# Moving work off the waits of a two-layer decoder trunk, and narrowing its last block

## The chip, the cores and the metric

The kernel runs on one core of one Trainium2 chip. A time is the device time of one execution in microseconds (us); several runs of the same kernel are summed up by their median. The profile comes from one execution of its own, taken by the hardware profiler. Engines are named as in it: PE is TensorE's matmuls, PEld its weight loads, DVE is VectorE, ACT is ScalarE, POOL is GpSimd, SP is SyncE, which issues the DMA transfers. An engine takes its instructions strictly in the order in which they stand in its queue.

## The reference, cut to what matters

One sequence of 1024 tokens with 1024 features goes through a Mamba-2 layer, a shared K/V projection, a stick-breaking attention layer and a last RMS norm:

```python
c_act = silu(c)
shift, scale, gate = split(c_act @ ada_w[0] + ada_b[0], 3)
h = rmsnorm(x, norm_g[0]) * (1 + scale) + shift
zxbcdt = h @ m_in_w                        # z 2048, x/B/C 3072, dt 32
xbc = silu(causal_dwconv(xbc) + conv_b)    # 4 taps
y = ssd_chunked(xs, dt, -exp(a_log), B, C) # 8 chunks of 128, 32 heads
#   per chunk: exp(acum_t - acum_s) below the diagonal * (C B^T), times xs
y = groupnorm((y + d_skip * xs) * silu(z)) * m_norm_g
x = x + gate * (y @ m_out_w)
k, v = split(modulate(x, kv...) @ kv_w, 2)
q, z = split(modulate(x, ada 1...) @ sb_in_w, 2)
x = x + gate1 * ((stick_breaking(q, k, v) * silu(z)) @ sb_out_w)
return rmsnorm(x, final_g)
```

All of it is in float32. The modulation products are the rows of `c_act @ ada_w`.

## The kernel before, in words

Every large product is split in three: an operand is rounded to a short float32 form (`hi`, a cast on ACT) and its remainder (`lo`, a subtraction on DVE or POOL), and `mm3` (L128 to L131) adds hi\*hi, hi\*lo and lo\*hi in PSUM. Weights come as tiles of 128 x 1024 by `load_w` (L116 to L126): a DMA into a raw buffer, the cast on L123, the subtraction on L124. PE takes a weight load of 128 columns before every matmul.

**Start** (L198 to L349). The order of PE, ACT, POOL and DVE is written out by hand here. The rows of x come in eight tiles of 128 tokens, `xn[0]` to `xn[7]`. `squares` (L200) sums the squares of one tile, on ACT or on DVE by its number; `rms` turns four sums into factors, `scaled` (L217) applies them. Per slice of 128 features `d` and half of the tokens `hf`, `turn` (L252) transposes on PE, `high` (L258) applies the modulation and rounds on ACT, `low` (L266) subtracts on DVE, and `wave_mm` (L270) multiplies with the first three weight tiles. `gemv` (L224) makes one slice of shift and scale on DVE, `bias` (L245) finishes it on ACT. `spin` (L210) issues matmuls whose result is overwritten.

**Convolution** (L341 to L458). 24 column tiles of x, B and C: 48 matmuls of 512 columns each, then `conv` (L345): one ACT operation, three on DVE, a SiLU on ACT (L353), a store. `ada_rest(i)` (L357) makes the other six modulation vectors, each from eight DMAs of 512 KB, on DVE (L366) or on POOL and ACT (L363, L364). A scheduler places these instructions by the program's order, what is ready, and its own estimate of durations.

**Scan** (L461 to L640). PE's order is by hand, the other engines' by the scheduler. `chunk_a` (L495) loads a 128 x 8 x 128 tile `lm` of sums of dt\*a, masks it on POOL (L512), and takes eight exponentials of 128 x 128 on ACT (L515); then it is multiplied with C B^T (L534). `chunk_b` (L537) uses it as an operand of `yd` (L545). `lm` has three buffers, so the first three chunks' tiles are loaded ahead. SiLU and the exponential use different ACT tables; a change costs an `ACT_TABLE_LOAD`.

**Attention and the end** (L752 to L1037). The last product with `wso` goes in three blocks of tokens, (half, first column, last column): (1, 0, 512), (0, 0, 256), (0, 256, 512). In a block, for each of eight feature tiles: 24 matmuls into `ps`, a DVE operation that adds the residual (L1009), a square on ACT (L1016), a sum on POOL (L1018). Then a product with ones (L1026, L1027), `inv_rms` (two on ACT, three on DVE), and the scaling: by `finish` (L961) beside the next block, and for the last block by three instructions at L1033, one on POOL and two on DVE, each with its output DMA (L1035).

Of the kernel before, what the change touches and what calls it, by code (L numbers as in the profile page):

```python
# [24 lines left out]
HT = T // NH  # L25
# [27 lines left out]
def tile_trunk(ctx, tc, xT, xN, c, vec, ada0, adar, wxbc, wwave, wdt, wz, wmo, wk, wv, wq, wqz, wso, out):  # L53
# [104 lines left out]
    with ExitStack() as es:  # L158
# [41 lines left out]
        def squares(t):  # L200
            sq = tp.tile([P, D], F32, tag="sq", name=f"sq{t}", bufs=2)
            acc = ssq[:, t // CPH, t % CPH:t % CPH + 1]
            if t % 2:
                V.scalar_tensor_tensor(out=sq, in0=xn[t], scalar=1.0, in1=xn[t], op0=ALU.mult,
                                       op1=ALU.mult, accum_out=acc)
            else:
                S.activation(sq, xn[t], AF.Square, accum_out=acc)
# [67 lines left out]
        def unit(d, hf):  # L275
            high(d, hf)
            low(d, hf)
# [11 lines left out]
        for t in range(CPH):  # L289
# [5 lines left out]
        gemv(0)  # L295
        V.scalar_tensor_tensor(out=vv("b_sc0"), in0=vv("b_sc0"), scalar=1.0, in1=vv("g0"), op0=ALU.add,
                               op1=ALU.mult)
        bias(0)
        unit(0, 0)
        wave_mm(0, 0)  # L300
        spin(xn[0][:, 0:HT], 3)
        for t in range(CPH, NC_):
            squares(t)
        rms(1)
        for t in range(CPH, NC_):
            scaled(t)
# [142 lines left out]
        for n, m in enumerate(todo):  # L449
            wh, wl = wnext if n == 0 else load_w(wxbc[m], f"x{m}")  # L450
            ps = pp.tile([P, T], F32, tag="pr", name=f"pr{m}")
            for k in range(ND):
                for hf in range(NH):
                    mm3(ps[:, hf * HT:(hf + 1) * HT], wh[:, k, :], wl[:, k, :], *h0[k][hf],
                        k == 0, k == ND - 1)
            conv(m, ps)
            if n >= 3 and n % 3 == 0 and n // 3 <= 6:
                ada_rest(n // 3 - 1)  # L458

# [2 lines left out]
    with ExitStack() as es:  # L464
# [32 lines left out]
        def chunk_a(u, c):  # L497
            g, xg, bt, ct = u["g"], u["xg"], u["bt"], u["ct"]
            n = f"{g}_{c}"
            h0_ = HPG * g  # L500
            hsl = slice(h0_, h0_ + HPG)
            cs = slice((c % CPH) * P, (c % CPH + 1) * P)
            sh3 = [P, HPG, P]
            r0 = c * 32 + h0_
            lm = pq.tile(sh3, F32, tag="lm", name="lm" + n, bufs=3)
            Y.dma_start(out=lm, in_=ac_d[r0:r0 + 8, :].rearrange("h t -> (h t)").partition_broadcast(P)
                        .rearrange("p (h t) -> p h t", t=P))
            eb = pq.tile([P, 4, P], F32, tag="eb", name="eb" + n, bufs=1)
            ev = ea_d[r0:r0 + 8, :].rearrange("(j a) t -> a j t", a=2)
            for a in range(2):  # L510
                Y.dma_start(out=eb[64 * a:64 * a + 64], in_=ev[a].partition_broadcast(64))
            Q.affine_select(out=lm, in_=lm, pattern=[[0, HPG], [1, P]], compare_op=ALU.is_ge,  # L512
                            fill=-1e30, base=0, channel_multiplier=-1)
            for h in range(HPG):
                S.activation(lm[:, h, :], lm[:, h, :], AF.Exp, bias=nac[:, c, h0_ + h:h0_ + h + 1])  # L515
            px = ppt.tile([P, 512], F32, tag="px", name="px" + n)
            for j in range(4):
                E.transpose(px[:, j * P:(j + 1) * P], xg[:, j, cs], ident)
            pb = ppt.tile([P, 512], F32, tag="pb", name="pb" + n, bufs=2)
            E.transpose(pb[:, 0:P], bt[:, cs], ident)  # L520
            E.matmul(pb[:, P:2 * P], bt[:, cs], ct[:, cs], start=True, stop=True)
            px3 = px.rearrange("p (h k) -> p h k", k=64)
            xd = pq.tile([P, HPG, 64], F32, tag="xd", name="xd" + n)
            V.tensor_tensor(out=xd, in0=px3, op=ALU.mult,
                            in1=dtv[:, c, hsl].unsqueeze(2).to_broadcast([P, HPG, 64]))
            sp = {}
            if c < NC_ - 1:
                xw = py.tile([P, HPG, 64], F32, tag="xw", name="xw" + n)
                V.tensor_tensor(out=xw, in0=px3, op=ALU.mult,
                                in1=wdv[:, c, hsl].unsqueeze(2).to_broadcast([P, HPG, 64]))  # L530
                sp["xw"] = xw.rearrange("p h k -> p (h k)")
                sp["bs"] = py.tile([P, P], F32, tag="bs", name="bs" + n)
                S.copy(sp["bs"], pb[:, 0:P])
            V.tensor_tensor(out=lm, in0=pb[:, P:2 * P].unsqueeze(1).to_broadcast(sh3), in1=lm, op=ALU.mult)  # L534
            return sp, xd, lm, eb
# [410 lines left out]
    with ExitStack() as es:  # L946
# [23 lines left out]
        w7 = load_w(wso[:, :, 7, :].rearrange("d p c -> p d c"), "s7")  # L970
        done = iter(())
        for hf, c0, c1, ds in ((1, 0, 512, (0, 5, 1, 2, 3, 4, 6, 7)), (0, 0, 256, (6, 7, 0, 1, 2, 3, 4, 5)),
                               (0, 256, 512, (6, 7, 0, 1, 2, 3, 4, 5))):
            w = c1 - c0
            last = hf == 0 and c0 > 0
            n = f"{hf}_{c0}"
            sh = [P, w]
            sqs = pf.tile(sh, F32, tag="sqs", name="sqs2_" + n)
            pss = pp.tile([P, HT], F32, tag="ss", name="ss2_" + n)[:, 0:w]
            x2 = []  # L980
            if hf == 0:
                x2t = pf.tile([P, 8, w], F32, tag="x2q", name="x2_" + n)
            for i, d in enumerate(ds):
                if hf == 0:
                    t = x2t[:, i, :]
                elif d < NPRE:
                    t = x2p[d]
                else:
                    t = pf.tile(sh, F32, tag=f"x2_{d}", name=f"x2_{d}", bufs=1)
                if hf == 0 or d >= NPRE:  # L990
                    Y.dma_start(out=t, in_=x1_d[d][hf][:, c0:c1])
                if hf == 1 and d == NPRE:
                    ps = part[d][0]
                elif hf == 1 and d < NPRE:
                    ps = mm_tile(f"ps{d}_{n}")
                else:
                    ps = pp.tile([P, HT], F32, tag="pq", name=f"ps{d}_{n}", bufs=4)[:, 0:w]
                if hf == 1 and d < NPRE:
                    mm3(ps, w7[0][:, d, :], w7[1][:, d, :], *gg[1][7], True, True)
                elif hf == 1 and d == NPRE:  # L1000
                    mm3(ps, part[d][1][:, 7, :], part[d][2][:, 7, :], *gg[1][7], False, True)
                else:
                    if d not in wos:
                        keep_w(d)
                    wh, wl = wos[d]
                    for k in range(ND):
                        h, l = gg[hf][k]
                        mm3(ps, wh[:, k, :], wl[:, k, :], h[:, c0:c1], l[:, c0:c1], k == 0, k == ND - 1)
                V.scalar_tensor_tensor(out=t, in0=ps, scalar=mod[:, GA1, d:d + 1], in1=t, op0=ALU.mult,  # L1009
                                       op1=ALU.add)  # L1010
                x2.append(t)
                if i == 0:
                    S.activation(sqs, t, AF.Square)
                else:
                    sq = pf.tile(sh, F32, tag="sq", name=f"sq2_{d}_{n}")
                    S.activation(sq, t, AF.Square)  # L1016
                    if i < ND - 1:
                        Q.tensor_tensor(out=sqs, in0=sqs, in1=sq, op=ALU.add)  # L1018
                if last:
                    S.activation(t, t, AF.Identity, scale=vv("gfin", d))  # L1020
                if hf == 1 and d == 4:
                    tc.keep_in_program_order(S.preload_act_table_set("natural_log_exp_and_others"))
                    for k in range(7):
                        load_gs(0, k)
                next(done, None)
            E.matmul(pss, ones, sqs, start=True, stop=False)  # L1026
            E.matmul(pss, ones, sq, start=False, stop=True)  # L1027
            r = pf.tile(sh, F32, tag="rb", name="rb2_" + n)
            inv_rms(pss, r, pf.tile(sh, F32, tag="sq", name="rt2_" + n), D)
            done = finish(hf, c0, c1, ds, x2, r)  # L1030
        for eng, i0, i1 in ((Q, 0, 2), (V, 2, 5), (V, 5, 8)):
            m = i1 - i0
            eng.tensor_tensor(out=x2t[:, i0:i1, :], in0=x2t[:, i0:i1, :],  # L1033
                              in1=r.unsqueeze(1).to_broadcast([P, m, w]), op=ALU.mult)
            Y.dma_start(out=out[ds[i0]:ds[i0] + m, :, c0:c1].rearrange("d p t -> p d t"),  # L1035
                        in_=x2t[:, i0:i1, :])
# [68 lines left out]
```

## Time and profile before

| what | value |
|---|---|
| median of 3 runs | 1477.11 us (1475.7 to 1477.21) |
| the profiled execution: time, span | 1481.88 us, 1480.2 us |
| PE busy | 1442.3 us, 97% of the span |
| PEld busy | 1112.3 us, 75% |
| DVE busy | 957.2 us, 65% |
| ACT busy | 726.7 us, 49% |
| POOL busy | 520.4 us, 35% |
| mean granted TensorE clock | 0.992 |

The span runs from the first to the last instruction that the profile shows. Busy time of PE says that matmuls are in flight, not how close together they are. The granted clock is a share of 2.4 GHz; 0.5 is 1.2 GHz.

### The profile page before, as it was taken

The page shows a single profiled execution, that of the slowest core. Times are in us where ns is not written, and L with a number is a line of the kernel's source. Part 1 is how long each engine was busy: PE and PEld are TensorE (multiplying, and loading weights), DVE is VectorE, ACT ScalarE, POOL GpSimd, SP SyncE. Part 2 cuts the span into 40 slices and gives each one's busy share as a digit, 9 for nine tenths or more (in the row PEclk, how much of TensorE's full clock was granted, in tenths as well). Part 3 has the DMA queues.
Part 4 walks back from the last instruction along what each step waited for, and adds up shares of the span by engine and source line. Part 5 has one row for each costly group of instructions (what it writes and reads, how often), then busy time and mean ns, then how long its engine had stood idle before and what let it go on. Part 6 is the DMA issues. An engine that isn't in the chain of part 4 may idle for free.

```text
span 1480.2 us, 20539 instructions
## 1 busy us (share of the span) xinstructions
PE 1442.3 (97%) x7580; PEld 1112.3 (75%) x7580; DVE 957.2 (65%) x1196; ACT 726.7 (49%) x1218; POOL 520.4 (35%) x602
## 2 busy tenths in 40 slices
PE   6999998999999999999999999999999999999997
PEld 3777886888777777778888888876666666666797
DVE  5688984454789889975733427326656665667564
ACT  6654535334666666733523325235545554555452
POOL 0012220001555655431011000037666666667532
PEclk9999999999999999999999999999999999999999
DMA  9368885224577766567433446441120212112253
GB/s 351 120 217 288 295 294 177 86 100 123 188 231 241 236 219 211 195 196 267 153 119 127 150 122 200 140 156 44 51 79 30 76 47 64 38 58 79 87 184 107
DMA packets 103395, 227.34 MB, mean 154 GB/s; under 512 B 9344, under 2 KB 40832, under 8 KB 102272
## 3 DMA queue, kind: packets, MB, share of 16 engines
q1 hardware_dynamic: 103296, 226.03, 45.8%
q8 instruction: 60, 0.98, 0.3%
q14 instruction: 39, 0.32, 0.1%
HBM read 184.32 MB, written 41.68 MB: 153 GB/s over the span
## 4 chain that ended last, share of the span: by engine, by line
PE 78%; DVE 3%; DMA 1%; ACT 1%; issue 1%; POOL 0%; DVEq 0%; SPq 0%; POOLq 0%; ACTq 0%
PE sc L829 5%; PE av L882 5%; PE at L861 4%; PE po L131 4%; PE po L130 4%; PE po L129 4%; PE pz L131 3%; PE pz L129 3%; PE pz L130 3%; PE pqz L129 2%; PE pq L129 2%; PE pr L131 2%; PE pq L131 2%; PE pr L129 2%; PE pr L130 2%; PE pq L130 2%
## 5 line engine op out<-in xcount | busy, mean ns | idle before, releaser
L852 POOL TENSOR_TENSOR be<-be,kp 128x1024 f32<-128x1024 f32 (+2 forms) x96 | 162.4, 1692 | 90.1 <-DVE kp L846 70.9
L832 ACT ACTIVATE kp<-sc 128x1024 f32<-128x1024 f32 (+2 forms) x96 | 75.6, 813 | 174.4 <-PE sc L829 171.8
L846 DVE TENSOR_TENSOR_SCAN kp<-kp,pone 128x128 f32<-128x128 f32 (+3 forms) x128 | 96.1, 802 | 69.2 <-POOL kp L839 69.2
L129 PE MATMUL pr<-h0h,hx 128*128 128x512 f32 x336 | 132.8, 395 | 7.1 <-ACT hx L123 4.0
L131 PE MATMUL pr<-h0h,lx 128*128 128x512 f32 x336 | 133.2, 396 | 1.4 <-DVE lx L124 1.4
L130 PE MATMUL pr<-h0l,hx 128*128 128x512 f32 x336 | 132.5, 394 | 0.0
L129 PE MATMUL pz<-h0h,hz 128*128 128x512 f32 x256 | 113.0, 441 | 0.0
L131 PE MATMUL po<-yh,lo 128*128 128x512 f32 x256 | 100.0, 391 | 1.3 <-DVE lo L124 1.3
L130 PE MATMUL po<-yl,ho 128*128 128x512 f32 x256 | 100.9, 394 | 0.3 <-DVE yl L659 0.3
L131 PE MATMUL pz<-h0h,lz 128*128 128x512 f32 x256 | 100.5, 393 | 0.1
L130 PE MATMUL pz<-h0l,hz 128*128 128x512 f32 x256 | 100.1, 391 | 0.0
L129 PE MATMUL po<-yh,ho 128*128 128x512 f32 x256 | 100.0, 391 | 0.0
L363 POOL TENSOR_TENSOR ar<-ar,crow 128x1024 f32<-128x1024 f32 x12 | 31.5, 2628 | 186.4 <-DMA ar<-adar 152.6
L846 DVE TENSOR_TENSOR_SCAN kp<-kp,ab,pone 128x512 f32<-128x512 f32 x64 | 78.3, 1265 | 28.3 <-ACT kp L832 17.2
L515 ACT ACTIVATE lm<-lm,nac 128x128 f32<-128x128 f32 x256 | 78.6, 390 | 36.3 <-POOL lm L512 35.9
L550 POOL TENSOR_TENSOR sd<-st,eev 128x512 f32<-128x512 f32 x24 | 39.4, 1641 | 133.7 <-ACT st L562 121.0
L124 POOL TENSOR_TENSOR lq<-rq,hq 128x256 fp32r<-128x256 f32 x32 | 22.4, 730 | 177.8 <-ACT hq L123 177.8
L829 PE MATMUL sc<-kd,q 64*128 64x512 f32 (+3 forms) x384 | 81.5, 522 | 0.8 <-ACT be L833 0.8
L350 DVE SCALAR_TENSOR_TENSOR cv<-pr,vt,cv 128x1023 f32<-128x1023 f32 (+2 forms) x63 | 80.3, 1277 | 0.9
L129 PEld LDWEIGHTS pr<-h0h,hx 128*128 128x128 f32 x336 | 64.2, 191 | 21.6 <-ACT hx L123 4.4
L512 POOL TENSOR_SCALAR_AFFINE_SELECT lm<-lm 128x1024 f32<-128x1024 f32 x32 | 40.3, 1260 | 113.2 <-DMA lm<-ac_d 84.4
L861 PE MATMUL at<-ident,be 128*128 128x128 f32 x576 | 74.7, 272 | 1.2 <-DVE aT L871 1.2
(257 smaller groups left out, 3814.2 us busy)
## 6 DMA issues: line engine op xcount, KB each, us to landing
ar<-adar SPq DMA_DIRECT2D x48, 512.0 KB, 5.6
lm<-ac_d SPq DMA_DIRECT2D x32, 512.0 KB, 4.8
rz<-wz SPq DMA_DIRECT2D x32, 512.0 KB, 3.6
ro<-wmo SPq DMA_DIRECT2D x32, 512.0 KB, 3.6
xs_d<-sv SPq DMA_DIRECT2D x24, 512.0 KB, 3.8
rx<-wxbc SPq DMA_DIRECT2D x21, 512.0 KB, 4.6
a<-ada SPq DMA_DIRECT2D x8, 1024.0 KB, 10.2
xg<-xs_d SPq DMA_DIRECT2D x8, 1024.0 KB, 5.8
```

The source lines that it names most:

```text
L129: E.matmul(ps, wh, xh, start=first, stop=False)
L130: E.matmul(ps, wh, xl, start=False, stop=False)
L131: E.matmul(ps, wl, xh, start=False, stop=last)
L350: V.scalar_tensor_tensor(out=ac[:, i:], in0=ps[:, :T - i], scalar=vv("cw", m * 4 + 3 - i), in1=ac[:, i:], op0=ALU.mult, op1=ALU.add)
L512: Q.affine_select(out=lm, in_=lm, pattern=[[0, HPG], [1, P]], compare_op=ALU.is_ge, fill=-1e30, base=0, channel_multiplier=-1)
L515: S.activation(lm[:, h, :], lm[:, h, :], AF.Exp, bias=nac[:, c, h0_ + h:h0_ + h + 1])
L829: E.matmul(ps[:, a, o:o + w], q[hsl[a], i * P:(i + 1) * P], kd[hsl[a], HT * c:HT * c + w], start=True, stop=True)
L832: S.activation(kp[:, :, ok:ok + w], ps[:, :, o:o + w], AF.Sigmoid, scale=-0.125)
L846: V.tensor_tensor_scan(out=ka, data0=ka, data1=pone.to_broadcast([P, w]), initial=1.0 if top else above[p, i][:, a, 0:1], op0=ALU.mult, op ...
L852: Q.tensor_tensor(out=be[:, :, o:o + w], in0=be[:, :, o:o + w], in1=kp[:, :, ok + 1:ok + w + 1], op=ALU.mult)
L861: E.transpose(ps[:, j, :], be[:, a, j * P:(j + 1) * P], ident)
L882: E.matmul(ps[hsl[a], cs], vd[:, j, hsl[a]], at[j // 4][:, a, j % 4, cs], start=j == 0, stop=j == nj - 1)
```

## The change

It has four parts. The squares of x tiles 4 and 5 go ahead of the first `bias`, those of tiles 6 and 7 between `high` and `low`, and tile 5 goes from DVE to ACT. The exponentials of the first three scan chunks keep their place in the program's order, behind the convolution. The calls of `ada_rest` stand behind other column tiles. The last block of 256 tokens becomes two of 128, with the last scaling in two DVE instructions instead of one on POOL and two on DVE.

```diff
         def squares(t):
-            if t % 2:
+            if t in (1, 3, NC_ - 1):
                 V.scalar_tensor_tensor(out=sq, in0=xn[t], scalar=1.0, in1=xn[t], op0=ALU.mult,
                                        op1=ALU.mult, accum_out=acc)
...
+        for t in (CPH, CPH + 1):
+            squares(t)
         bias(0)
-        unit(0, 0)
+        high(0, 0)
+        for t in (CPH + 2, CPH + 3):
+            squares(t)
+        low(0, 0)
         wave_mm(0, 0)
         spin(xn[0][:, 0:HT], 3)
-        for t in range(CPH, NC_):
-            squares(t)
         rms(1)
...
             conv(m, ps)
-            if n >= 3 and n % 3 == 0 and n // 3 <= 6:
-                ada_rest(n // 3 - 1)
+            if n in (5, 8, 11, 13, 15, 17):
+                ada_rest((5, 8, 11, 13, 15, 17).index(n))
...
             for h in range(HPG):
-                S.activation(lm[:, h, :], lm[:, h, :], AF.Exp, bias=nac[:, c, h0_ + h:h0_ + h + 1])
+                e = S.activation(lm[:, h, :], lm[:, h, :], AF.Exp, bias=nac[:, c, h0_ + h:h0_ + h + 1])
+                if g == 0 and c < 3:
+                    tc.keep_in_program_order(e)
...
-                               (0, 256, 512, (6, 7, 0, 1, 2, 3, 4, 5))):
+                               (0, 256, 384, (6, 7, 0, 1, 2, 3, 4, 5)), (0, 384, 512, tuple(range(8)))):
             w = c1 - c0
-            last = hf == 0 and c0 > 0
+            last = hf == 0 and c1 == HT
...
-        for eng, i0, i1 in ((Q, 0, 2), (V, 2, 5), (V, 5, 8)):
+        for eng, i0, i1 in ((V, 0, 4), (V, 4, 8)):
             m = i1 - i0
             eng.tensor_tensor(out=x2t[:, i0:i1, :], in0=x2t[:, i0:i1, :],
                               in1=r.unsqueeze(1).to_broadcast([P, m, w]), op=ALU.mult)
```

Line numbers in the changed kernel are higher by 3 behind the start, and by 5 behind the exponentials.

ACT's queue at the start, before; `sq` are the squares of an x tile, `mod` is `bias(0)`, `hx` and `h0h` are `high(0, 0)`, `rst` begins `rms(1)`:

```order
L233 CAST wwh_263<-ww_185 128x384
L246 ACTIVATE mod<-mod,vt 128x1
L248 ACTIVATE mod<-mod,vt 128x1
L260 ACTIVATE hx_0_0_272<-xp_0_250,mod 128x512
L263 CAST h0h_0_274<-hx_0_0_272 128x512
L207 ACTIVATE sq_290,ssq<-x_174 128x1024
L207 ACTIVATE sq_294,ssq<-x_176 128x1024
L139 ACTIVATE rst<-ssq,epsb 128x4
```

And of the change:

```order
L233 CAST wwh_263<-ww_185 128x384
L207 ACTIVATE sq_270,ssq<-x_174 128x1024
L207 ACTIVATE sq_272,ssq<-x_175 128x1024
L246 ACTIVATE mod<-mod,vt 128x1
L248 ACTIVATE mod<-mod,vt 128x1
L260 ACTIVATE hx_0_0_276<-xp_0_250,mod 128x512
L263 CAST h0h_0_278<-hx_0_0_276 128x512
L207 ACTIVATE sq_281,ssq<-x_176 128x1024
L139 ACTIVATE rst<-ssq,epsb 128x4
```

Two squares now stand ahead of `mod`, and one instead of two between `h0h` and `rst`; of DVE's two squares one is left, ahead of its `h0l`.

ACT's queue in the convolution, before; `sv` is a tile's SiLU, `lm_0` to `lm_2` are the exponentials of the first three chunks, `hx` is the cast of the next weights:

```order
L353 ACTIVATE sv_1569<-cv_1564 128x1024
L515 ACT_TABLE_LOAD
L515 ACTIVATE lm_0_2388<-lm_0_2388,nac 128x128 x8
L123 CAST hx_1727<-rx_1725 128x1024
L348 ACTIVATE cv_1627<-pr_1578,vt 128x1024
L515 ACTIVATE lm_1_2507<-lm_1_2507,nac 128x128 x8
L515 ACTIVATE lm_2_2583<-lm_2_2583,nac 128x128 x8
L353 ACT_TABLE_LOAD
L353 ACTIVATE sv_1632<-cv_1627 128x1024
L123 CAST hx_1790<-rx_1788 128x1024
```

In the change these exponentials stand at the start of the scan, between the casts of the z weights (`hz`) and the copies of z out of PSUM (`sz`):

```order
L482 COPY sz_0_2322<-pz_0_1_2362 128x512
L518 ACT_TABLE_LOAD
L518 ACTIVATE lm_0_2388<-lm_0_2388,nac 128x128 x8
L538 COPY bs_0_2416<-pb_0_2409 128x128
L123 CAST hz_0_0_2493<-rz_0_0_2491 128x1024
L518 ACTIVATE lm_1_2507<-lm_1_2507,nac 128x128 x3
L482 COPY sz_0_2322<-pz_0_2_2425 128x512
L518 ACTIVATE lm_1_2507<-lm_1_2507,nac 128x128 x5
L123 CAST hz_0_1_2569<-rz_0_1_2567 128x1024
L518 ACTIVATE lm_2_2583<-lm_2_2583,nac 128x128 x3
L482 COPY sz_0_2322<-pz_0_3_2457 128x512
L518 ACTIVATE lm_2_2583<-lm_2_2583,nac 128x128 x5
```

A table load, the SiLU of z and another table load follow. In the convolution nothing stands between the SiLU and the next cast any more. POOL's, DVE's and SP's queues in the convolution have the same instructions in the same order in both kernels, those of `ada_rest` among them.

PE's queue at the end, before: the last matmuls of the block of 256 and its product with ones.

```order
L130 MATMUL ps_0_256_12667<-gl_0_11900,hs_12392 128x256
L131 MATMUL ps_0_256_12667<-gh_0_11899,ls_12393 128x256
L1026 MATMUL ss_0_256_12435<-sqs_0_256_12434,ones 128x256
L1027 MATMUL ss_0_256_12435<-sq_5_0_256_12693,ones 128x256
L1100 UNCONDITIONAL_BRANCH
```

And of the change, at the place where the first block of 128 hands over to the second:

```order
L131 MATMUL ps_0_384_12703<-gh_0_12029,ls_12203 128x128
L129 MATMUL ps_0_384_12703<-gh_0_12035,hs_12202 128x128
L130 MATMUL ps_0_384_12703<-gl_0_12036,hs_12202 128x128
L1031 MATMUL ss_0_256_12435<-sqs_0_256_12434,ones 128x128
L131 MATMUL ps_0_384_12703<-gh_0_12035,ls_12203 128x128
```

The 192 matmuls of 256 columns behind the block (0, 0, 256) have become 384 of 128 columns, with one more pair of products with ones. On SP eight loads of 128 x 128 for the second block follow the stores of the block (0, 0, 256).

## Rows read from the trace of the kernel before

**Rows 1.** The page, chain of work that ended last: shares of the span by engine

```profile
PE 78%; DVE 3%; DMA 1%; ACT 1%; issue 1%; POOL 0%; DVEq 0%; SPq 0%; POOLq 0%; ACTq 0%
```

**Rows 2.** Waits of PE: for whom, us in total, times, longest

```profile
PE pr L129 <- ACT hx L123: 4.0, 1, 4.0
PE prw L129 <- ACT h0h L263: 3.5, 2, 2.0
PE prw L130 <- DVE h0l L268: 2.8, 5, 1.4
PE pr L131 <- DVE lx L124: 1.4, 1, 1.4
```

**Rows 3.** Timeline of ACT, start: start us, us, instruction [idle before <-releaser]

```profile
18.61 0.39 ACT L246 ACTIVATE mod<-mod,vt 128x1 f32<-128x1 f32 x1 [3.00 <-DVE vt L296]
...
21.72 1.06 ACT L207 ACTIVATE sq<-x 128x1024 f32<-128x1024 f32 x1
...
23.87 0.30 ACT L139 ACTIVATE rst<-ssq,epsb 128x4 f32<-128x4 f32 x1 [1.00 <-DVE sq L204]
```

**Rows 4.** Timeline of DVE and PE at the first wave

```profile
30.41 0.69 DVE L268 TENSOR_TENSOR h0l<-hx,h0h 128x512 fp32r<-128x512 f32 x1
...
31.15 0.80 PE L130 MATMUL prw<-h0l,wwh 128*128 128x512 f32 x1 [1.42 <-DVE h0l L268]
...
36.87 0.45 PE L129 MATMUL prw<-h0h,wwh 128*128 128x512 f32 x1
```

**Rows 5.** Timeline of ACT in the convolution

```profile
223.66 1.06 ACT L353 ACTIVATE sv<-cv 128x1024 f32<-128x1024 f32 x1 [2.79 <-issue]
...
230.33 2.44 ACT L515 ACTIVATE lm<-lm,nac 128x128 f32<-128x128 f32 x8 [4.31 <-POOL lm L512]
232.68 1.03 ACT L123 CAST hx<-rx 128x1024 fp32r<-128x1024 f32 x1
```

**Rows 6.** Timeline of PE, the same place

```profile
222.11 0.39 PE L129 MATMUL pr<-h0h,hx 128*128 128x512 f32 x1
...
229.36 0.39 PE L131 MATMUL pr<-h0h,lx 128*128 128x512 f32 x1
233.76 0.50 PE L129 MATMUL pr<-h0h,hx 128*128 128x512 f32 x1 [4.01 <-ACT hx L123]
...
241.61 0.47 PE L129 MATMUL pr<-h0h,hx 128*128 128x512 f32 x1
```

**Rows 7.** Windows of 2 us: busy time per engine (instructions), granted clock, DMA

```profile
236.00:238.00 2.00, 2.00 (x5) 1.61 (x6) 1.97 (x2) 2.00 (x8) 0.00 (x0) 0.50 0.53 141
```

**Rows 8.** DMA issues from 205 to 222 us: KB each, median us to landing

```profile
rx<-wxbc SPq DMA_DIRECT2D x2, 512.0 KB, 4.4
```

**Rows 9.** The chain in order of time, start of the scan: start us, us, what

```profile
353.01 1.02 PE yd L545 x16
...
362.39 1.09 PE yo L555 x8
```

**Rows 10.** Timeline of PE, matmuls of 256 columns in the last block

```profile
1469.09 0.28 PE L129 MATMUL ps<-gh,hs 128*128 128x256 f32 x1
1469.21 0.28 PE L130 MATMUL ps<-gl,hs 128*128 128x256 f32 x1
```

**Rows 11.** Timeline of PEld, two weight loads at the head of a group

```profile
1007.70 0.19 PEld L129 LDWEIGHTS pq<-h1h,hq 128*128 128x128 f32 x1
1007.81 0.19 PEld L130 LDWEIGHTS pq<-h1l,hq 128*128 128x128 f32 x1
```

**Rows 12.** Timeline of the end, all engines

```profile
1469.65 0.48 DVE L1009 SCALAR_TENSOR_TENSOR x<-ps,mod,x 128x256 f32<-128x256 f32 x1 [2.40 <-PE ps L131]
...
1473.38 0.42 DVE L146 SCALAR_TENSOR_TENSOR rb<-rt,rb 128x256 f32<-128x256 f32 x1
...
1473.88 2.03 POOL L1033 TENSOR_TENSOR x<-x,rb 128x512 f32<-128x512 f32 x1 [5.24 <-DVE rb L146]
```

**Rows 13.** Groups by line, L1033: ns min/median/max, first and last start

```profile
L1033 DVE TENSOR_TENSOR x<-x,rb x2: 958/1486/2015, 1473.8 to 1474.7; 128x768 f32<-128x768 f32 x2
```

## The prediction

> **What bounds the kernel now.** I read the chain of work that ended last first: 78% of the span is PE, and no other engine has more than 3% [rows 1]. The kernel is one long row of matmuls. A change can win time where PE stands still or runs at the half clock, or where it needs fewer or cheaper matmuls; it can lose where it makes them dearer. Next I read for whom PE waits: the longest single wait is 4.0 us for an ACT cast of weights, `hx` L123, and behind it come 3.5 us in two waits for `h0h`, 2.8 us in five for `h0l`, and 1.4 us for `lx` [rows 2]. All of these lie at the start and in the convolution. Then I read each place of the change in the timeline of the engines there.
>
> **Pace of PE.** From the matmul at 222.11 to that at 229.36 [rows 6] there are 32, so one of 512 columns takes 7.25/32 = 0.227 us. In the last block the starts of two matmuls of 256 columns lie 1469.21 − 1469.09 = 0.12 us apart [rows 10].
>
> **The first scan exponentials.** On ACT the cast `hx` at 232.68 stands behind eight exponentials at 230.33, and these waited 4.31 us for POOL's mask of `lm` [rows 5]. So PE, which needs the cast, stood from 229.59 to 233.76 (its wait is given as 4.01 us, and the matmul at 229.36 would have been followed 0.23 us later) [rows 6]. That is 4.17 us. What follows is dearer still: from 233.76 to 241.61 PE issued 15 matmuls in 7.85 us [rows 6], where 15 × 0.227 = 3.41 would do; the granted clock there is 0.50, that is 1.2 GHz [rows 7]. That is 4.44 us more. With the exponentials gone from here the cast can follow the SiLU, which ends at 223.66 + 1.06 = 224.72 [rows 5]. Its raw weights are there: of the two transfers the median lands 4.4 us after its issue, the issues lie from 205 to 222 us [rows 8], and this tile's was issued before 222, seven us ahead of its use. So `hx` ends at some 225.8, the subtraction some 1.4 us later, ahead of 229.59. I take both parts, 4.17 + 4.44 = **8.6 us**. The lower bound is the waits alone, 4.0 + 1.4 = 5.4 us [rows 2], if the clock falls in spite of that; the upper is 8.8, with the wait for `lx` beside it.
>
> The same 24 exponentials then cost 3 × 2.44 = 7.3 us on ACT at the start of the scan, and the two table loads move with them. PE's chain there passes through `yd` from 353.01 and `yo` at 362.39 [rows 9]; the first needs `lm` of chunk 0. In ACT's new order these eight stand right behind the second copy of z, ahead of the copy of the first chunk's B, so they come well before 353; those of chunks 1 and 2 stand between casts and copies of z that PE needs later. What hides them is the z product, which PE works through in that time. I cost the place at nothing; the bounds are 0 and 8.6, which is what the same instructions cost where they stood (rival C).
>
> **The other modulation products.** The queues of POOL, DVE and SP in the convolution are the same in both kernels, and what waits there is data from the same transfers. 0 us: this part does not do what its lines say.
>
> **The start.** ACT waits 3.00 us, until 18.61, for `vt` from DVE [rows 3]. Two squares of 1.06 us with 0.1 between them fit in, since x tiles 4 and 5 have landed. Of the two on ACT that stood behind `high`, one is left, and of the two on DVE one. Before, `rms(1)` began at 23.87 after 1.00 us of waiting for DVE's second square [rows 3]. Now DVE's one square ends about 20.3 and ACT's third about 21.7, one square earlier, so `rms(1)` begins at 21.75: 2.1 us earlier. What waits for it on PE is the second half of the tokens: PE waited 1.42 us for `h0l` until 31.15 [rows 4]. This `h0l` also hangs on `gemv(1)` on DVE, which frees earlier by one square, so I take 1.8 of the 2.1 us. The matmul at 36.87 still takes 0.45 us, that at 222.11 took 0.39 and the one at 31.15 took 0.80 [rows 4, 6]: I read the stretch from 31 to 37 as the half clock. About 11 matmuls at 0.43 against 0.227 lose 2.2 us; if the idle time ahead of them shrinks, part of that comes back. Between 1.8 and 1.8 + 2.2 I take **3.0 us**; the bounds are 1.0 (a later wait takes the rest) and 5.
>
> **The last block.** Removed are 8 × 24 = 192 matmuls of 256 columns, 192 × 0.120 = 23.04 us. Added are 2 × 8 × 24 = 384 of 128 columns, each with a weight load of its own as before. The weights are the same, so they are loaded twice. The price of one has no row with this type and width. From below: columns alone. 256 columns more cost 0.227 − 0.120 = 0.107 us, so 128 fewer than 256 cost 0.0535 less, 0.0665. From above: `yo`, eight f32 matmuls of 128 columns in 1.09 us [rows 9], where one product takes two of these, is 0.2725 a product. Between them: the weight load. Two at the head of a group, with no matmul to wait for, start 1007.81 − 1007.70 = 0.11 us apart [rows 11], and a load stands before each matmul whatever its width. At 256 columns the load hides under 0.120; at 128 it is the longer of the two. I take 0.110: 384 × 0.110 = 42.24, so **+19.2 us**. The bounds of the whole are thus +2.5 (0.0665) and +81.6 (0.2725); the nearest row is the load's, and if what goes with it lets the pace be 0.107 to 0.120 the term is +18.0 to +23.0. The extra product with ones is four f32 matmuls of 0.11: **+0.45**. The eight extra loads of x on SP stand behind the stores of block (0, 0, 256) and are wanted only some 20 us later, behind the first block of 128: hidden.
>
> The Trainium skill ("TensorE: Matmul & The Clock Gate", section "Back-to-back issue gap") gives about 81 ns for each matmul of 128 columns in a sustained stream of load and matmul pairs; the trace has no such stream of this width, and by that figure the estimate would be 384 × 0.081 = 31.1 us, +8.1 in place of +19.2, and the sum −5.6, about 1471.5. It speaks against the 0.110 of the loads, which is a row of this kernel, and the row decides.
>
> **The end.** Behind the last matmul stand, for 256 columns, the residual (0.48), square, product, two on ACT, and three of DVE at 0.42 [rows 12]. With 128 columns each of DVE's drops by some 0.15 (its first scaling took 0.958 for 768 columns [rows 13], 0.16 for 128): four times that is 0.6, and I add 0.4 for ACT's three and PE's product, which shrink alike: 1.0 us. The scaling: DVE's two of 768 columns took 0.958 and 2.015, the second beside POOL's one of 2.03 [rows 12, 13]; together 2.97 us. Now two of 8 × 128 / 2 = 512 columns each run without POOL: 2 × 0.958 × 512/768 = 1.28, with a little between them 1.4. That is 1.5 us less. Together **2.5 us**; bounds 1.5 (DVE keeps its mean pace of 1.49 per 768, so 2.0 for both) and 3.5.
>
> **Sum.** −8.6 − 3.0 + 19.2 + 0.45 − 2.5 = **+5.55 us**. Against the profiled execution's own 1481.88 that is 1487.4. This execution lies 4.77 us above the median of the runs, 1477.11; the same step from there gives 1482.7.
>
> **Rivals.**
> A: narrow matmuls go by their columns. PE would start the next 128 columns while the load for a later one is under way, and loads come faster than the 0.11 us seen at a group's head. Price 0.0665: 384 × 0.0665 = 25.5, +2.5, and the sum is −11.2: 1465.9, faster. For it: at 256 and 512 columns pace goes by columns. Against it: loads at least 0.11 apart [rows 11]; it decides from a pace under 0.0955 us, where 384 × 0.0955 − 23.04 = 13.65 eats up what the other terms (−8.6 − 3.0 − 2.5 + 0.45) save.
> B: narrow products cost what f32 products do, 0.2725 each: 384 × 0.2725 = 104.6, +81.6, and about +68: 1545. For it: the only matmuls of 128 columns with float32 operands in the trace go so [rows 9]. Against it: those are of the full type in two passes, these of the short one in one.
> C: the exponentials cost PE at the start of the scan what they cost in the convolution. `lm` of chunk 0 is then later than 353.01 or the state copies later than 362.39 [rows 9]; the gain of 8.6 is gone and the sum is +14.15: 1491.3. Against it: ACT's order, in which chunk 0's eight come first.
>
> **How the numbers follow.** Forecast .70, A .15 (with prices between 0.0665 and 0.09), B .07, C .08. What a measurement can tell from no change is 0.2%, 2.95 us. The forecast's own range: load-bound pace +18 to +23, exponentials −8.8 to −5.4, start −5 to −1, end −3.5 to −1.5; not all at one end, 1478 to 1492. To hold 8 in 10, the range goes down to 1462 for most of A and up to 1493 for C; B is left out. Faster: A and the gain end of the forecast, .20. Slower: most of the forecast, B, C, .71. Within: .09.
>
> **What would show it.** Right: in the convolution no PE wait for `hx` near 229 us, and no clock of 0.50 near 236; `rms(1)` about 2 us earlier and PE's first wait for `h0l` shorter; in the two blocks of 128 matmul starts 0.11 us apart, the stretch of both 42 us long with PEld busy throughout; the scaling at the end in 1.4 us. Wrong: starts 0.07 apart (A) or 0.27 (B); a new wait of `yd` or `yo` for ACT between 340 and 365 us (C); or a wait for `hx` or `lx` at the next tile that takes the place of the one removed, which would show as a PE gap of over 1 us between 230 and 260 us.

## The result and the profile after

| comparison | before, median (runs) | changed, median (runs) | ratio, 95% interval |
|---|---|---|---|
| first | 1477.16 us (4) | 1488.11 us (4) | 1.0073, 1.0057 to 1.0089 |
| second, on another chip | 1477.39 us (23) | 1488.58 us (6) | 1.0065, 1.0047 to 1.0083 |

The changed kernel is slower by some 11 us, 0.7%. The forecast said slower, by 5.55 us: the direction and the largest term were right, the size was half. Between the two profiled executions the difference is 1485.9 − 1480.2 = 5.7 us, as forecast; between the medians it is twice that. The profiled execution of before was a long one (1481.88 us against a median of 1477.16), which the first experiment shows in its stages.

The chain of work that ended last in the changed kernel, shares of the span (before in [rows 1]):

```profile
PE 88%; DVE 6%; ACT 2%; DMA 2%; issue 2%; POOL 0%; SPq 0%; DVEq 0%; ACTq 0%; POOLq 0%
```

PE's waits, in total, times, longest. The wait for the cast `hx` (4.0 in [rows 2]) and that for `lx` are not among them any more; `h0h` has 1.8 instead of 3.5, `h0l` 1.6 instead of 2.8. The longest in the convolution is now a single wait of 2.9 us for `cv`, the convolution on DVE; it is not new, before it came to 3.1 us in two:

```profile
PE pr L129 <- DVE cv L353: 2.9, 1, 2.9
PE prw L129 <- ACT h0h L263: 1.8, 2, 1.5
PE prw L130 <- DVE h0l L268: 1.6, 5, 0.4
```

The start in the timeline of the changed kernel. ACT fits two squares into its wait (0.90 us are left of the 3.00 in [rows 3]), `rst` begins at 21.69 and not at 23.87, and PE's matmul that waited for `h0l` until 31.15 [rows 4] starts at 28.97:

```profile
16.54 1.04 ACT L207 ACTIVATE sq<-x 128x1024 f32<-128x1024 f32 x1
...
18.57 0.39 ACT L246 ACTIVATE mod<-mod,vt 128x1 f32<-128x1 f32 x1 [0.90 <-DVE vt L296]
...
21.69 0.30 ACT L139 ACTIVATE rst<-ssq,epsb 128x4 f32<-128x4 f32 x1
...
28.97 0.50 PE L130 MATMUL prw<-h0l,wwh 128*128 128x512 f32 x1 [0.43 <-DVE h0l L268]
```

The convolution, where PE stood for the cast [rows 5, 6]. The SiLU is followed by a cast with nothing between, and this cast is already that of the tile after; PE runs on at 0.227 us, with the clock at 1.00 in the window that had 0.50 in [rows 7]:

```profile
223.21 1.06 ACT L356 ACTIVATE sv<-cv 128x1024 f32<-128x1024 f32 x1 [4.07 <-issue]
225.53 1.05 ACT L123 CAST hx<-rx 128x1024 fp32r<-128x1024 f32 x1 [1.25 <-PE pr L130]
...
226.01 0.39 PE L131 MATMUL pr<-h0h,lx 128*128 128x512 f32 x1
226.23 0.39 PE L129 MATMUL pr<-h0h,hx 128*128 128x512 f32 x1
```

```profile
236.00:238.00 2.00, 2.00 (x10) 1.67 (x9) 0.51 (x1) 1.59 (x2) 0.00 (x0) 1.00 0.00 0
```

The narrow blocks. Matmuls of 128 columns start 0.11 to 0.12 us apart, as do their weight loads, where those of 256 columns took 0.12 [rows 10]. At the change-over the loads keep their distance (1433.34, 1433.46, 1433.57), but the second narrow matmul starts only 0.06 us behind the first; from then on the matmuls follow their loads. From the first (1433.46) to the last (1477.49) it is 44.03 us for 384; before it was 23.78 for 192. The mean is 44.03/384 = 0.115, which contains the products with ones between them; without those it is 0.112, the median 0.111:

```profile
1433.46 0.22 PE L129 MATMUL ps<-gh,hs 128*128 128x128 f32 x1
1433.52 0.28 PE L130 MATMUL ps<-gl,hs 128*128 128x128 f32 x1
1433.63 0.27 PE L131 MATMUL ps<-gh,ls 128*128 128x128 f32 x1
...
1477.15 0.28 PE L131 MATMUL ps<-gh,ls 128*128 128x128 f32 x1
1477.20 0.19 PEld L129 LDWEIGHTS ps<-gh,hs 128*128 128x128 f32 x1
1477.26 0.28 PE L129 MATMUL ps<-gh,hs 128*128 128x128 f32 x1
1477.32 0.19 PEld L130 LDWEIGHTS ps<-gl,hs 128*128 128x128 f32 x1
1477.38 0.27 PE L130 MATMUL ps<-gl,hs 128*128 128x128 f32 x1
...
1477.49 0.27 PE L131 MATMUL ps<-gh,ls 128*128 128x128 f32 x1
```

The last scaling, two of 512 columns without POOL beside them, takes 1.29 us; before, the two of 768 took 0.958 and 2.015 [rows 13], with POOL's at work beside both (1473.88 to 1475.91 [rows 12]):

```profile
L1038 DVE TENSOR_TENSOR x<-x,rb x2: 685/688/692, 1481.0 to 1481.6; 128x512 f32<-128x512 f32 x2
```

### The profile page after: what moved, and what is told of

Its sections match the earlier page's. It is cut to its first block, busy times and chain, and to the rows that moved or that the text cites. A ratio compares the mean times of both kernels' runs of the same rounds, so it can differ in the third digit from the quotient of the medians.

```text
span 1485.9 us, 21021 instructions
## 1 busy us (share of the span) xinstructions
PE 1458.6 (98%) x7776; PEld 1131.0 (76%) x7776; DVE 957.1 (64%) x1213; ACT 728.7 (49%) x1230; POOL 518.4 (35%) x607
## 3 DMA queue, kind: packets, MB, share of 16 engines
q8 instruction: 62, 1.02, 0.3%
## 4 chain that ended last, share of the span: by engine, by line
PE 88%; DVE 6%; ACT 2%; DMA 2%; issue 2%; POOL 0%; SPq 0%; DVEq 0%; ACTq 0%; POOLq 0%
PE sc L834 5%; PE av L887 5%; PE pr L129 4%; PE pr L131 4%; PE pr L130 4%; PE at L866 4%; PE po L131 4%; PE po L130 4%; PE po L129 4%; PE pz L129 3%; PE pz L130 3%; PE pz L131 3%; PE pqz L129 2%; PE pq L129 2%; PE pq L131 2%; PE pq L130 2%
```

## The experiments

Times of before vary from 1471 to 1485 us in these comparisons, so each run stands against before in the same comparison, by its ratio. The diffs are against before unless another kernel is named.

**1. Before again.** No edit.

> The kernel before, unchanged, so that its stalls in the convolution are seen in further executions. Theory (the profiled execution of before was a long one, because the stretch at half clock behind the wait for the weights has no fixed length): the times lie between 1475 and 1482 us, most near 1477, and this trace shows the wait of 4.2 us near 229 us again, but a shorter stretch at half clock somewhere, some 3 to 5 us less in all than the trace of before. Rival (the profiled execution is simply longer everywhere): the same stretches at half clock, and the difference spread over the span.

Measured: 1476.37 us (12 runs, 1473.2 to 1479.0), ratio 0.9988, 0.9971 to 1.0004. In its trace the mask of `lm` begins at 224.15 and not at 229.20; the cast follows at 227.63 and not at 232.68 [rows 5], and PE waits 0.48 and 0.53 us where it waited 4.01 and 1.4 [rows 2, 6]. The clock stays at 1.00:

```profile
224.15 1.09 POOL L512 TENSOR_SCALAR_AFFINE_SELECT lm<-lm 128x1024 f32<-128x1024 f32 x1 [8.58 <-DMA lm<-ac_d]
...
227.63 1.03 ACT L123 CAST hx<-rx 128x1024 fp32r<-128x1024 f32 x1
...
228.72 0.50 PE L129 MATMUL pr<-h0h,hx 128*128 128x512 f32 x1 [0.48 <-ACT hx L123]
...
229.98 0.50 PE L131 MATMUL pr<-h0h,lx 128*128 128x512 f32 x1 [0.53 <-DVE lx L124]
```

```profile
231.00:233.00 2.00, 2.00 (x10) 1.65 (x9) 1.93 (x3) 2.00 (x8) 0.00 (x0) 1.00 0.73 250
```

So the expected wait of 4.2 us was not seen again: not only the half clock has no fixed length, the wait itself has none. It hangs on when a DMA lands, against where PE is by then. The rival is out: of the 6.3 us by which this span is shorter than that of before, 1.2 lie ahead of the convolution and 7.5 in it, and behind it this execution is the longer one.

**2. Exponentials alone.**

```diff
-                S.activation(lm[:, h, :], lm[:, h, :], AF.Exp, bias=nac[:, c, h0_ + h:h0_ + h + 1])
+                e = S.activation(lm[:, h, :], lm[:, h, :], AF.Exp, bias=nac[:, c, h0_ + h:h0_ + h + 1])
+                if g == 0 and c < 3:
+                    tc.keep_in_program_order(e)
```

> Only the exponentials of the first three chunks are kept in program order. Theory (they take away the wait of PE for the weight cast and the half clock behind it, and cost nothing in the scan): 4.2 us of waiting and between 2 and 4.4 us of half clock go, 1469 to 1471 us against 1477; yd and yo show no new wait. Rival (the half clock follows elsewhere, or the scan pays for it): above 1474 us.

Measured: 1474.91 us (12 runs), ratio 0.9974, 0.9956 to 0.9992: 1.2 to 6.5 us faster, and not the 8.6 of the forecast, nor the expected 6 to 8. By its time, above 1474 us, the rival came in; but before stood at 1479 in this comparison, and against that the gain lies between the two. The convolution has no wait for `hx`, but this execution has a wait of 2.22 us in the scan, with half clock behind it:

```profile
475.29 1.46 PE L596 MATMUL rs<-sq,ones 128*128 128x512 f32 x2 [2.22 <-POOL sq L588]
```

```profile
476.00:478.00 2.00, 2.00 (x13) 1.32 (x14) 1.51 (x3) 0.70 (x3) 2.00 (x2) 0.50 0.51 97
```

**3. Squares alone.** The two hunks of the change in the start.

> Only the squares at the start are moved. Theory: the second half of the tokens is ready earlier, 1.8 us of PE's wait goes and with it part of the half clock, in sum 3 us: 1474 us. Rival (what the trace of after shows at the start is a matter of how long the half clock happened to last): within 1 us of before, though the wait for h0l at 31 us is gone.

Measured: 1472.99 us (12 runs), ratio 0.9970, 0.9951 to 0.9989: 1.6 to 7.2 us faster. The first matmul of the convolution starts at 76.17, in before at 80.90 and in run 1 at 79.70: the theory holds. Its trace still has the exponentials in the convolution, and PE's wait for the cast has a third length:

```profile
PE pr L129 <- ACT hx L123: 2.4, 1, 2.4
```

**4. Narrow block alone.** The hunks of the last block and of the last scaling.

> Only the last block is cut in two of 128 tokens, with the last scaling in two DVE instructions. Theory (a matmul of 128 columns is paced by its weight load, 0.112 us): 384 x 0.112 - 23.0 = +20, +0.6 for the product with ones, -2.1 at the end: 1495 to 1496 us. Rival (pace by columns, 0.0665): +1 us, 1478.

Measured: 1494.68 us (6 runs), ratio 1.0121, 1.0095 to 1.0148: +14 to +22 us; its 384 matmuls take 44.03 us as well. The theory holds, and pace by columns is out. Here the wait for the cast was a fourth length:

```profile
PE pr L129 <- ACT hx L123: 0.7, 1, 0.7
```

**5. Exponentials and squares, without the narrow block.** The hunks of 2 and 3 together.

> The change without its narrow last block: exponentials kept in program order and squares moved, the last block as before. Theory (the two gains add as measured apart, -4 and -5 us, since the wait for the weight cast has another length in every execution and the forecast took the longest): 1469 to 1471 us where before is 1478, and the times spread less than those of before. Rival (the forecast's -8.6 for the exponentials holds once the start is in order): 1466 us.

Measured: 1471.85 us (12 runs; before 1476.40 in 34), ratio 0.9969, 0.9956 to 0.9981: 2.8 to 6.5 us faster. This version beats both kernels. The times lie between 1469.7 and 1473.5; those of before in the same comparison between 1472.3 and 1484.7, so the spread is smaller, as expected. That the two gains add is not shown: 7 to 9 us were expected and 4.6 measured, where runs 2 and 3 gave 3.9 and 4.4 apart. The three intervals are too wide to tell. The rival's 1466 us is out.

**6. The same with the last scaling on DVE alone.** Against run 5:

```diff
-                               (0, 256, 512, (6, 7, 0, 1, 2, 3, 4, 5))):
+                               (0, 256, 512, tuple(range(8)))):
...
-        for eng, i0, i1 in ((Q, 0, 2), (V, 2, 5), (V, 5, 8)):
+        for eng, i0, i1 in ((V, 0, 4), (V, 4, 8)):
```

> As the run with exponentials and squares, and the last block of 256 scaled at the end by two DVE instructions of four tiles each, in the order 0 to 7. Theory: two of 1024 columns take 2 x 1.3 = 2.6 us instead of 2.9 with POOL beside them: 0 to 0.5 us faster than that run. Rival (the order 0 to 7 makes the last block wait for weights or x): slower than that run by over 2 us.

Measured: 1471.01 us (12 runs), ratio 0.9964, 0.9949 to 0.9978. Not to be told from run 5, and no cost of the order 0 to 7 shows. In the traces the scaling takes 2.36 us against 2.89 in run 5, but the span ends 9.47 us behind the last product with ones, against 9.16: what the scaling gains does not reach the end.

**7 and 8. A cast late in every execution, bare and filled.** Against run 5; the second of the hunks in run 8 only. `rep` is 12 for the tile n == 13 and 1 for every other:

```diff
-            S.copy(h[:, i:i + n, :], r[:, i:i + n, :])
+            for _ in range(rep):
+                S.copy(h[:, i:i + n, :], r[:, i:i + n, :])
...
+            if n == 13:
+                for _ in range(18):
+                    E.matmul(ps[:, 0:HT], h0[0][0][0][:, 0:P], h0[0][0][0], start=True, stop=True)
```

> Exponentials and squares as in the run before, and the weight cast at which PE stood in the profile of before is made twelve times over on ACT, so that it is late in every execution. Theory (a wait of some 4 us costs its own length, some 1.4 us for the subtraction behind it, and a stretch at 1.2 GHz behind both): 4.2 + 1.4 of waiting and 1.5 to 3.5 us of half clock, 7 to 9 us over the run with exponentials and squares, and the trace shows the granted clock at 0.5 right behind the wait. Rival (the half clock has nothing to do with the wait): 5.5 us over it, clock 1.0 behind the wait.

> The same late cast, with 18 matmuls of 512 columns whose result is overwritten in front of the waiting one. Theory: they fill 18 x 0.227 = 4.1 us of the wait, the granted clock stays at 1.0, and only the wait itself is paid: 1.5 to 3.5 us less than the run with the late cast alone. Rival (the half clock comes from elsewhere): the same time as that run within 1 us, clock at 0.5 as there.

Measured: 1482.09 us (12 runs), 1.0031 (1.0016 to 1.0047), and 1482.68 us (11 runs), 1.0039 (1.0026 to 1.0053). The first is 10.2 us over run 5, more than the 7 to 9 expected. Between the two there is no difference, but the pair did not test what it should: the wait was 8.95 us and not 4.2, and behind the 18 matmuls PE still waited 3.27 and 1.12 us. Inconclusive, so it was made again with nine casts and 24 matmuls.

**9. The changed kernel again.** No edit.

> The changed kernel, unchanged, so that its time and that of before are compared over many executions. Theory (the narrow block costs 44.0 - 23.8 = 20.2 us in the trace, the end gives 2, and the exponentials and squares give 4 to 5): 1487 to 1490 us, 10 to 14 us over before. Rival (the first comparison caught before in its short executions, and the forecast's +5.5 holds): 1482 to 1484 us.

Measured: the second row of the table of results, +11.2 us between medians. The theory holds.

**10. Four blocks of 64.** Against the changed kernel: the two blocks from 256 to 512 become four, (256, 320), (320, 384), (384, 448), (448, 512).

> The changed kernel with the last block in four of 64 tokens instead of two of 128. Theory (the weight load of 128 columns sets the pace, not the width of the product): 768 matmuls at 0.11 us again, 84 to 86 us for the stretch instead of 44, +42 with the products with ones, less 1 at the end: about 1529 us. Rival (the pace falls with the columns): at 0.06 us 46 us for the stretch, about 1492 us.

Measured: 1606.82 us (4 runs), ratio 1.0872, 1.0846 to 1.0897. Slower than either theory. At first matmuls of 64 columns are 0.11 us apart, no nearer than those of 128: the load sets the pace. Then the granted clock goes to 0.50 and stays there until the end, though PE has no gap, and loads are 0.21 us apart, so that 768 take 163.6 us:

```profile
1434.79 0.28 PE L129 MATMUL ps<-gh,hs 128*128 128x64 f32 x1
...
1434.90 0.28 PE L130 MATMUL ps<-gl,hs 128*128 128x64 f32 x1
...
1435.02 0.28 PE L131 MATMUL ps<-gh,ls 128*128 128x64 f32 x1
...
1500.18 0.33 PEld L129 LDWEIGHTS ps<-gh,hs 128*128 128x128 f32 x1
1500.39 0.33 PEld L130 LDWEIGHTS ps<-gl,hs 128*128 128x128 f32 x1
```

```profile
1434.00:1436.00 2.00, 2.00 (x20) 2.00 (x20) 1.70 (x3) 0.60 (x2) 0.40 (x2) 1.00 0.70 264
1440.00:1442.00 2.00, 2.00 (x11) 2.00 (x11) 0.61 (x2) 0.98 (x3) 0.00 (x0) 0.50 0.00 0
1500.00:1502.00 2.00, 2.00 (x12) 2.00 (x11) 0.00 (x0) 0.00 (x0) 0.00 (x0) 0.50 0.00 0
```

**11 and 12. The late cast with nine in place of twelve, bare and behind 24 matmuls.**

> As the run with the late cast, with nine casts in place of twelve, so that the wait of PE is about 4 to 5 us and not 9. Theory (a wait costs its own length and a stretch at 1.2 GHz behind it): 5 to 6 us of waiting with the subtraction, 1.5 to 3.5 us of half clock, 1478 to 1480 us, clock 0.5 behind the wait in the trace. Rival (no half clock behind a wait of this length): 1476 to 1477 us.

> The same nine casts, and 24 matmuls whose result is overwritten, 24 x 0.227 = 5.4 us, in front of the waiting one. Theory: PE has no gap of over 1 us near 230 us and the clock stays at 1.0; the wait is paid, the half clock is not: 1.5 to 3.5 us less than the run with nine casts alone. Rival: the same time within 1 us.

Measured: 1477.93 us (12 runs), 1.0003 (0.9987 to 1.0019), and 1477.74 us (12 runs), 0.9995 (0.9981 to 1.0008). The first is at the edge of the theory's 1478, the second by its time is the rival's. In the bare one PE waits 6.21 us and ten matmuls then take 237.03 − 232.60 = 4.43 us where 2.27 would do:

```profile
226.01 0.39 PE L132 MATMUL pr<-h0h,lx 128*128 128x512 f32 x1
232.60 0.80 PE L130 MATMUL pr<-h0h,hx 128*128 128x512 f32 x1 [6.21 <-ACT hx L124]
...
237.03 0.47 PE L132 MATMUL pr<-h0h,lx 128*128 128x512 f32 x1
```

```profile
233.00:235.00 2.00, 2.00 (x6) 1.52 (x6) 2.00 (x3) 0.65 (x1) 0.00 (x0) 0.50 0.06 16
```

In the filled one there is no gap and no half clock:

```profile
226.08 5.60 PE L458 MATMUL pr<-h0h 128*128 128x512 f32 x24
231.52 0.39 PE L130 MATMUL pr<-h0h,hx 128*128 128x512 f32 x1
```

```profile
233.00:235.00 2.00, 2.00 (x11) 1.65 (x10) 1.97 (x3) 0.00 (x0) 0.00 (x0) 1.00 0.88 266
```

The convolution is 3.4 us shorter in the filled trace (241.00 against 244.44 us from its first matmul to its last). So in this pair of traces the clock falls at a wait and does not where PE is kept at work. The other traces agree. In brackets are PE's waits for this cast and its subtraction, and with them the clock was at 0.50 for no time in run 1 (0.48 and 0.53 us) and run 4 (0.73 and 1.32), for 3.4 us in run 3 (2.43 and 1.42), for 6.8 in before (4.01 and 1.40), run 8 (3.27 and 1.12) and run 11 (6.21), and for 10.2 in run 7 (8.95). In the medians the filling gains nothing that shows: 0.2 us. The filled trace has a stretch at half clock of 3.4 us from 619.47 on that the bare one has not. Whether that is so in most executions stays open.

## Why the prediction was right or wrong

The measured 1488 us lies in the forecast's own range, 1478 to 1492, some 5 us above its value. The stages of ten traces (all but those of the late casts) tell which term was mis-sized. The table takes the first and last matmul of the convolution (`pr`), and the first of the last product (`ps`). "In" and "out" say whether the exponentials stand in the convolution.

| trace | until convolution | convolution | from there to last product |
|---|---|---|---|
| before (in) | 80.90 | 244.25 | 1081.34 |
| 1 before again (in) | 79.70 | 236.79 | 1083.70 |
| 4 narrow alone (in) | 79.79 | 238.42 | 1080.94 |
| 3 squares alone (in) | 76.17 | 240.68 | 1080.41 |
| 2 exponentials alone (out) | 80.34 | 235.59 | 1085.63 |
| 5 both (out) | 76.22 | 236.17 | 1085.08 |
| 6 both, DVE scaling (out) | 76.01 | 235.19 | 1082.07 |
| after (out) | 77.36 | 235.01 | 1081.40 |
| 9 after again (out) | 77.37 | 235.87 | 1081.69 |
| 10 quarters (out) | 76.39 | 235.88 | 1082.19 |

**The exponentials: the term that was mis-sized.** The forecast took 4.17 + 4.44 = 8.6 us from one wait and the half clock behind it. With the exponentials in, the convolution takes 244.25, 236.79, 238.42, 240.68, in the mean 240.0; with them out 235.0 to 236.2, mean 235.6. The term is −4.4 and not −8.6: of four executions the profiled one had the longest wait (4.0, against 0.5, 0.7, 2.4). The mechanism was right, the wait for the cast is gone in every trace without them. For the execution from which it was read the size was about right as well: its convolution is 9.2 us longer than that of the changed kernel (244.25 against 235.01). What was wrong is "the same step from there", which carried the gain over to the median of runs; in none of the other three traces was this much to be won. That the sum came within 0.2 us of the difference between the two profiled executions, 5.7 us, is therefore no proof of its size for the medians. Why the mask came 5 us later in that one execution is not settled; its DMA was issued some 4 us later (221.75 against 217.63 in run 1), and SP's queue was already 3.4 us behind at 126 us.

**Their place in the scan** was costed at nothing. The third column is 1080.4 to 1083.7 (mean 1081.6) with them in, 1081.4 to 1085.6 (mean 1083.0) with them out. The forecast's bounds hold, and rival C's sign is absent: in no trace does PE wait for over 0.1 us between 320 and 375 us. That 1.4 us is a cost of the place is not shown. The long ones in the table (1083.7, 1085.6, 1085.1) are those in which the clock fell to half for 3.4 us in this stretch, which costs about half of that; the rest lies in waits far behind the exponentials, in run 2 1.47 us for `lm` at 464 and 2.22 us for `sq` at 475. Run 7, not in the table, has 1084.4 without a fall of the clock there.

**The start** was forecast at −3.0 and gave 76.6 against 80.2 us in the mean of the first column, −3.6. `rms(1)` came 2.2 us earlier, as worked out (2.1), PE's `h0l` 2.2 (1.8 forecast).

**The narrow block** was +19.2 + 0.45 = +19.65, and the last product, from its first matmul to its last, now takes 83.56 in the median of runs 4, 9 and after (83.56, 83.28, 83.72) against 62.83, +20.7. Of the 1.05 us between them, 0.6 lie in the two blocks themselves (44.03 − 23.78 = 20.25), where the pace was 0.112 in the mean, not 0.110, and the rest ahead of them. That the load sets the pace, and rivals A and B are wrong, was right: run 4 shows it alone; in run 10 half the columns come no faster; and at the change-over two matmuls of 128 columns started 0.06 us apart while the loads stayed 0.11 to 0.12 apart, so it is not the matmuls that ask for 0.11. Rival B's ground was misread: `yo` is not the only matmul of 128 columns with float32 operands, and `yd` in the same rows, with 64 columns of weights, has sixteen in 1.02 us [rows 9], 0.13 a product and not 0.27. The figure of the Trainium skill ("TensorE: Matmul & The Clock Gate", section "Back-to-back issue gap") of about 81 ns at 128 columns does not hold for this stream of load and matmul pairs: 0.111 us in the median was measured.

**The end** was −2.5 and is 1.69 + 9.18 − 1.33 − 7.08 = 2.46 us less (from the last matmul of `ps` to the last product with ones, and from there to the end of the span). The forecast took 0.958 us for 768 columns as DVE's pace without POOL; POOL was at work beside that scaling too, but the pace held: 1.29 us for the two of 512 columns, where it had 1.28, or 1.4 with a little between them.

**The other modulation products** were forecast at nothing. This was not run by itself, but the convolution takes as long with the lines changed (235.0, 235.9, 235.9) as without (235.6, 236.2, 235.2).

The sum by what was measured: −4.4 + 1.4 − 3.6 + 20.7 − 2.5 = +11.6, against +11.2 between medians. Of the 6.05 us by which this sum lies above the forecast, 4.2 are the exponentials, 1.4 the scan, 1.05 the narrow block, and −0.6 the start. Without the scan's 1.4, whose cause is not shown, the sum is +10.2.

## What to carry to other kernels

A wait in a profile is one draw. Where it ends with a DMA that is issued behind much else, look at it in two or three executions before its length goes into a sum, and subtract it from the execution in which it was seen, not from the median. Narrowing a block shortens what stands behind the last matmul by a few us, but once the weight load sets the pace, a matmul gets no cheaper by being narrower (here 0.111 us at 128 columns and at 64), so that the halved block pays for each half in full: here 20 us for 2.5.

## What the runs showed of the hardware that was not expected

A stream of matmuls without any gap can itself lose the clock: 64 columns with a weight load each ran at 1.2 GHz from 1438 us to the end of run 10, while 128 columns kept 2.4 GHz for 44 us; why is not shown. And the same wait is not always followed by the half clock. PE waits 1.26 us for `lo` in run 1 and 1.27 in the changed kernel; in the first the clock falls within a microsecond, in the second it does not. This wait is there in all 14 traces, with 1.24 to 1.27 us, and the fall behind it in three (runs 1, 5 and 12). Run 1:

```profile
617.27 0.50 PE L131 MATMUL po<-yh,lo 128*128 128x512 f32 x1 [1.26 <-DVE lo L124]
```

```profile
618.00:620.00 2.00, 2.00 (x7) 1.50 (x6) 2.00 (x4) 1.18 (x4) 2.00 (x2) 0.50 0.69 250
```

The changed kernel:

```profile
612.50 0.50 PE L131 MATMUL po<-yh,lo 128*128 128x512 f32 x1 [1.27 <-DVE lo L124]
```

```profile
613.00:615.00 2.00, 2.00 (x11) 1.60 (x10) 2.00 (x5) 0.63 (x3) 1.75 (x2) 1.00 0.80 214
```
